# A mixing layer's triangular inverses: blocks of 16 rows on VectorE, joined to 32 by products on TensorE

## The chip, the cores and the metric

The kernel runs on one core of a Trainium2 chip. Its time is the device time of one execution in microseconds (us). All arrays are fp32. Matrix products run on TensorE (PE in the profile, PEld is its weight loading), element-wise work on VectorE (DVE), ScalarE (ACT) and GpSimd (POOL); the sync engine (SP) issues the DMAs.

## The reference, cut to what matters

Four layers, each of token mixing (two recurrent branches over 256 context and 256 latent tokens, in two directions) and a dense channel mixer. The change lies in the second branch, whose state update is a delta rule:

```python
def step(S, xt):
    w_t, k_t, b_t, kk_t, v_t = xt[:5]
    sa = -jnp.einsum('...vk,...k->...v', S, kk_t)
    S = S * w_t[..., None, :] + sa[..., None] * b_t[..., None, :] + v_t[..., None] * k_t[..., None, :]
    if not read:
        return S, None
    return S, jnp.einsum('...vk,...k->...v', S, xt[5])
```

The kernel computes it in chunks of 64 tokens. Within a chunk, each token's correction depends on all earlier ones, so each chunk needs the inverse of a 64 by 64 triangular matrix with a unit diagonal: I minus a strictly triangular part.

## The kernel before, in words

All work is first recorded as a program and then put in order by a list scheduler (`Plan.schedule`), which gives each engine a fixed order of instructions before the kernel is built, from costs and ranks of its own. On the chip each engine goes through its order strictly, so an instruction that must wait holds up everything behind it on its engine. `plan.together` keeps several matmuls in one piece of that order.

A layer has two parts. In the **mixing stage** the projections of the input (tile `p_ps`, three split products for each weight) run beside two recurrent branches. The **tail** after it (output projections and channel mixer) is nearly all products of 512 columns.

The delta-rule branch handles its 8 heads as 4 pairs p = 0 to 3. For each pair three streams are recorded:

- `rw_pair(p)` computes decays, keys and so on, and from them the triangular matrices ("ZA", in the memory of tile `AR`) and the scores (`SC`).
- `rw_solve(p)` inverts 32 matrices of a pair at once (2 directions, 8 chunks, 2 heads).
- `rw_chain(p)` goes through the 8 chunks one after another: products on `c_ps`, copies by ScalarE, state updates by VectorE (`UV<-c_ps`, `S<-c_ps`). It needs the scores and the inverses of its pair. The chain of pair p runs beside the solve of pair p + 1.

`rw_solve` cuts each 64 by 64 matrix into two diagonal blocks of 32 and one block off the diagonal. The 64 diagonal blocks (32 matrices, 2 blocks each) are laid out with one block to a partition: 64 partitions with 32 by 32 values each, in `LT` (the tile's memory is `XS`), by two transposes in blocks of 32 (`XS<-AR`). Then comes the elimination: for i = 30 down to 1 one multiplication into a scratch area in `S` (`S<-XS`) and one addition (`XS<-XS,S`) on (31 - i) x i values in each partition, 60 dependent VectorE instructions. Two transposes (`AR<-XS`) and one more (`XS<-AR`) bring the inverted blocks back, and TensorE joins the two blocks of 32 to 64 by two products of 32 by 32 per matrix (`s_ps<-AR,XS`, `s_ps<-XS,AR`), with ScalarE copies out of PSUM between them. The tag `s` of PSUM has two buffers, which the scores, the transposes and the small projections of the mixing stage share.

```python
tv = tmp[:, 0:n * i].rearrange("p (c j) -> p c j", j=i)
vec.tensor_tensor(out=tv, in0=Lp[:, i + 1:32, i:i + 1].to_broadcast([C, n, i]),
                  in1=Lp[:, i:i + 1, 0:i].to_broadcast([C, n, i]), op=ALU.mult)
vec.tensor_tensor(out=Lp[:, i + 1:32, 0:i], in0=Lp[:, i + 1:32, 0:i], in1=tv, op=ALU.add)
```

Nearly every instruction is recorded through one helper, so the profile gives line 343 for all of them; they are told apart by tiles. A product of fp32 operands shows as two matmul records in the trace.

Of the kernel before, what the change touches and what calls it, by code (L numbers as in the profile page):

```python
# [12 lines left out]
AF = mybir.ActivationFunctionType  # L13
ALU = mybir.AluOpType
# [15 lines left out]
C = 64  # L30
# [62 lines left out]
class Plan:  # L93
# [104 lines left out]
    def cost(eng, name, out, args, kw):  # L198
# [31 lines left out]
        if name == "tensor_scalar":  # L230
            if ptr:
# [7 lines left out]
               act=dict(pe=230.0, act=145.0, vec=143.0, pool=170.0, dma=200.0),  # L239
               vec=dict(pe=245.0, act=130.0, vec=127.0, pool=130.0, dma=200.0),  # L240
# [113 lines left out]
def body(ctx, tc, xT, cc, ada_w, w_in, rw_lo, rw_g2, proj_a, proj_b, w_out, ffn_w1, ffn_w2,  # L354
         vecs, lbl, c_id, c_bo, c_sc, c_hg, c_sh, out, depth=4):
    nc = tc.nc
    plan = Plan(nc, tc)
    vec, act, pool, pe, dma = plan.vec, plan.act, plan.pool, plan.pe, plan.dma
# [13 lines left out]
    def st(tag, shape, dt=F32, bufs=1):  # L372
        return plan.tile(sp, shape, dt, tag, 2 if tag in B2 else bufs, tag)
# [24 lines left out]
    def sps(tag="s"):  # L398
        return plan.tile(pss, [P, 512], F32, tag, PSB[tag], tag + "_ps")
# [344 lines left out]
    def layer(l, pm, xs, xd, hh, hl):  # L744
# [59 lines left out]
        SX = st("S", [P, 1024])  # L804
        S = SX[:, 0:512].rearrange("p (d s c) -> p d s c", d=2, s=4)
        ar3 = MX[:, 0:3072].rearrange("p (w d s c) -> p d s w c", w=3, d=2, s=NCH)
        LT = MX[:, 3072:4096]
# [177 lines left out]
        def rw_solve(p):  # L985

            yield lambda: ("za" if EA[last] else "grp", p) in flags
            yield lambda: p == 0 or ("sol", p - 1) in flags
            yield ("at", par["ps"][p] + par["pz"])
            z, o = C * (p % 2), C - C * (p % 2)  # L990
            za = ZA.rearrange("p d s h c -> p (d s h) c")
            ZZ = za[z:z + C]
            Zq = [ZZ[32 * q:32 * q + 32] for q in range(2)]
            Lp = LT[o:o + C].rearrange("p (c j) -> p c j", j=32)
            T1 = LT[z:z + 32].rearrange("p (n c) -> p n c", c=32)
            Hs = LT[z + 32:z + C].rearrange("p (n c) -> p n c", c=32)
            tmp = SX[o:o + C, 512:768]
            for q in range(2):
                vec.transpose(Lp[32 * q:32 * q + 32], Zq[q][:, :, 32 * q:32 * q + 32].rearrange("p n i -> p i n"))
            for i in range(30, 0, -1):  # L1000
                n = 31 - i
                tv = tmp[:, 0:n * i].rearrange("p (c j) -> p c j", j=i)
                vec.tensor_tensor(out=tv, in0=Lp[:, i + 1:32, i:i + 1].to_broadcast([C, n, i]),
                                  in1=Lp[:, i:i + 1, 0:i].to_broadcast([C, n, i]), op=ALU.mult)
                vec.tensor_tensor(out=Lp[:, i + 1:32, 0:i], in0=Lp[:, i + 1:32, 0:i], in1=tv, op=ALU.add)
                yield 1
            vec.memset(LT[o:o + C, 0:1024:33], 1.0)
            vec.memset(Zq[1][:, :, 0:32], 0.0)
            for q in range(2):
                vec.transpose(Zq[q][:, :, 32 * q:32 * q + 32].rearrange("p n c -> p c n"), Lp[32 * q:32 * q + 32])  # L1010
            vec.transpose(T1, Zq[0][:, :, 0:32])
            for hf in range(2):
                ps = sps()
                for i in range(16):
                    n = hf * 16 + i
                    pe.matmul(ps[z + 32:z + C, i * 32:(i + 1) * 32], Zq[0][:, n, 32:C], T1[:, n, :], start=True,
                              stop=True)
                act.activation(Hs[:, hf * 16:hf * 16 + 16, :],
                               ps[z + 32:z + C].rearrange("p (a c) -> p a c", a=16), AF.Copy)
                yield 1.5  # L1020
            for hf in range(2):
                ps = sps()
                for i in range(16):
                    n = hf * 16 + i
                    pe.matmul(ps[z:z + 32, i * 32:(i + 1) * 32], Hs[:, n, :], Zq[1][:, n, 32:C], start=True, stop=True)
                act.activation(Zq[0][:, hf * 16:hf * 16 + 16, 32:C],
                               ps[z:z + 32].rearrange("p (a c) -> p a c", a=16), AF.Copy)
                yield 1.5
            flags["sol", p] = 1
# [283 lines left out]
        for i in range(4):  # L1313
            run += [[0.0, 4 * i, f"P{i}", rw_pair(i), None], [0.0, 4 * i + 1, f"C{i}", rw_chain(i), None],
                    [0.0, 4 * i + 1.5, f"Z{i}", rw_solve(i), None],
                    [0.0, 4 * i + 2, f"H{i}", hg_head(i), None]]
# [208 lines left out]
```

## Time and profile before

| | us |
|---|---|
| median of 3 runs (4347.94 to 4358.15) | 4348.0 |
| the profiled execution, its own time | 4335.38 |
| its span, first to last instruction | 4333.6 |
| busy: PE / DVE / ACT / POOL | 3898.9 / 3248.5 / 2147.8 / 1901.6 |

The four mixing stages lie at about 60 to 660, 1205 to 1842, 2335 to 2985 and 3478 to 4060 us of the span. A PE that is busy is not one that works at its fastest, since the ends of pipelined matmuls are modelled: a second look at the time per product is needed.

### The profile page before, as it was taken

The page shows a single profiled execution, that of the slowest core. Times are in us where ns is not written, and L with a number is a line of the kernel's source. Part 1 is how long each engine was busy: PE and PEld are TensorE (multiplying, and loading weights), DVE is VectorE, ACT ScalarE, POOL GpSimd, SP SyncE. Part 2 cuts the span into 40 slices and gives each one's busy share as a digit, 9 for nine tenths or more (in the row PEclk, how much of TensorE's full clock was granted, in tenths as well). Part 3 has the DMA queues.
Part 4 walks back from the last instruction along what each step waited for, and adds up shares of the span by engine and source line. Part 5 has one row for each costly group of instructions (what it writes and reads, how often), then busy time and mean ns, then how long its engine had stood idle before and what let it go on. Part 6 is the DMA issues. An engine that isn't in the chain of part 4 may idle for free.

```text
span 4333.6 us, 71689 instructions
## 1 busy us (share of the span) xinstructions
PE 3898.9 (90%) x26290; PEld 3081.4 (71%) x26290; DVE 3248.5 (75%) x5759; ACT 2147.8 (50%) x4234; POOL 1901.6 (44%) x1622
## 2 busy tenths in 40 slices
PE   7898898799988988999998889899899987888898
PEld 4666666677776666778777767667777875676898
DVE  5988978977479899675536998987854289888665
ACT  4555653433255556534433556554444254566564
POOL 1343543456533435464553243444555433345332
PEclk8999899999998998999999989889999997798999
DMA  4211137455422111363444111116444331111555
GB/s 149 64 53 46 54 100 219 137 167 157 132 87 62 53 49 51 122 210 100 134 121 136 55 47 55 50 45 216 134 134 129 103 113 43 44 56 52 172 151 161
DMA packets 661409, 451.03 MB, mean 104 GB/s; under 512 B 28224, under 2 KB 584256, under 8 KB 661056
## 3 DMA queue, kind: packets, MB, share of 16 engines
q1 hardware_dynamic: 661056, 446.44, 34.6%
q8 instruction: 207, 3.39, 0.3%
q14 instruction: 146, 1.20, 0.1%
HBM read 416.98 MB, written 29.36 MB: 103 GB/s over the span
## 4 chain that ended last, share of the span: by engine, by line
PE 40%; DVE 18%; issue 3%; ACT 2%; DMA 1%; POOL 1%; DVEq 0%; SPq 0%; POOLq 0%; ACTq 0%
PE p_ps L343 31%; PE s_ps L343 4%; DVE XS L343 3%; PE c_ps L343 3%; PE g_ps L343 2%; DVE wl L343 2%; DVE S L343 2%; DVE AR L343 1%; DVE hX L343 1%; DVE UV L343 1%; DVE X8b L343 1%; DVE X8a L343 1%; DVE fn L343 1%; DVE y L343 1%; DVE og L343 1%
## 5 line engine op out<-in xcount | busy, mean ns | idle before, releaser
L343 PE MATMUL p_ps<-hh,wl 128*128 128x512 f32 (+1 forms) x2784 | 1057.9, 397 | 64.6 <-DVE wl L343 48.7
L343 PE MATMUL p_ps<-hh,wh 128*128 128x512 f32 (+1 forms) x2784 | 1062.5, 393 | 35.7 <-ACT wh L343 24.4
L343 PE MATMUL p_ps<-hl,wh 128*128 128x512 f32 (+1 forms) x2784 | 1055.4, 390 | 0.0
L343 ACT ACTIVATE wh<-wr 128x512 fp32r<-128x512 f32 x986 | 608.4, 621 | 812.7 <-PE p_ps L343 726.6
L343 POOL TENSOR_TENSOR wl<-wr,wh 128x512 fp32r<-128x512 f32 x492 | 673.2, 1371 | 696.5 <-ACT wh L343 501.9
L343 PEld LDWEIGHTS p_ps<-hh,wl 128*128 128x128 f32 x2784 | 539.1, 196 | 198.5 <-DVE wl L343 68.3
L343 PEld LDWEIGHTS p_ps<-hh,wh 128*128 128x128 f32 x2784 | 538.3, 196 | 144.3 <-ACT wh L343 37.0
L343 PEld LDWEIGHTS p_ps<-hl,wh 128*128 128x128 f32 x2784 | 538.9, 196 | 93.1 <-issue 6.2
L343 DVE TENSOR_TENSOR wl<-wr,wh 128x512 fp32r<-128x512 f32 (+1 forms) x494 | 364.8, 743 | 126.0 <-ACT wh L343 80.8
L343 POOL TENSOR_SCALAR fn<-fn 128x512 f32<-128x512 f32 (+1 forms) x152 | 230.9, 1519 | 249.3 <-ACT fn L343 232.2
L343 DVE TENSOR_TENSOR fn<-fn,p_ps 128x512 f32<-128x512 f32 (+1 forms) x208 | 127.4, 615 | 254.8 <-ACT fn L343 152.8
L343 POOL TENSOR_SCALAR S0P<-S,pcs 128x64 f32<-128x64 f32 x192 | 148.4, 791 | 345.1 <-DVE S L343 329.8
L343 ACT ACTIVATE fn<-fn 128x512 f32<-128x512 f32 (+1 forms) x304 | 174.4, 574 | 104.6 <-POOL fn L343 100.3
L343 POOL COPY SC<-XS 64x256 f32<-64x256 f32 x128 | 73.6, 575 | 327.7 <-DVE SC L343 321.9
L343 DVE TENSOR_TENSOR XS<-XS,S 64x30 f32<-64x30 f32 (+14 forms) x480 | 208.2, 434 | 11.3
L343 POOL TENSOR_TENSOR HB<-HB,HA 128x512 f32<-128x512 f32 x112 | 162.6, 1452 | 113.9 <-ACT hY L343 110.6
L343 DVE TENSOR_TENSOR S<-XS 64x30 f32<-64x30 f32 (+14 forms) x480 | 198.7, 414 | 11.1
L343 POOL TENSOR_TENSOR HA<-HA 128x512 f32<-128x512 f32 x112 | 144.4, 1289 | 19.7 <-ACT hX L343 14.0
L343 PE MATMUL p_ps<-SC,wh 128*128 128x512 f32 (+1 forms) x440 | 145.6, 367 | 6.4 <-ACT SC L343 4.3
L343 DVE SCALAR_TENSOR_TENSOR UV<-c_ps,pcs,S0P 64x64 f32<-64x64 f32 x384 | 108.6, 283 | 40.6 <-PE c_ps L343 31.1
L343 ACT ACTIVATE fn<-p_ps 128x512 f32<-128x512 f32 (+1 forms) x217 | 113.1, 521 | 50.9 <-PE p_ps L343 33.8
L343 POOL TENSOR_SCALAR X8a<-X8a 128x512 f32<-128x512 f32 x64 | 106.9, 1670 | 41.2 <-ACT X8a L343 38.7
(477 smaller groups left out, 8781.8 us busy)
## 6 DMA issues: line engine op xcount, KB each, us to landing
wr<-ffn_w SPq DMA_DIRECT2D x512, 256.0 KB, 3.0
wr<-w_in SPq DMA_DIRECT2D x408, 256.0 KB, 2.9
hq<-ada_w SPq DMA_DIRECT2D x242, 256.0 KB, 2.9
PB<-ada_w SPq DMA_DIRECT2D x110, 256.0 KB, 2.9
wr<-w_out SPq DMA_DIRECT2D x64, 256.0 KB, 3.3
gts<-fn SPq DMA_DIRECT2D x48, 256.0 KB, 3.1
wr<-proj_a SPq DMA_DIRECT2D x32, 256.0 KB, 3.7
wr<-proj_b SPq DMA_DIRECT2D x32, 256.0 KB, 4.2
```

The costliest lines, as they stand in the source:

```text
L343: getattr(self.eng[self.on[i]], name)(*args, **kw)
```

## The change

The elimination stops at blocks of 16 rows. Each partition's 32 by 32 block is treated as two diagonal blocks of 16, both in one instruction, by an access pattern with one more dimension (`blocks`): 14 steps of 2 x (15 - i) x i values in place of 30 of (31 - i) x i. The 16 by 16 block below the diagonal, which the elimination no longer reaches, is made by two products of 16 by 16 for each of the 64 blocks: first the block itself times one inverse, copied by ScalarE into scratch `G` (memory of `S`), then the other inverse times that, copied into the matrix. Three transposes (`S<-XS`, `XS<-XS`) lay the operands out for TensorE. A memset of a block that is already zero is dropped, and the products of the join of 32 to 64 now stand in groups (`plan.together`). The tables that steer the list scheduler are untouched, but it orders the whole new program anew.

```diff
-            for i in range(30, 0, -1):
-                n = 31 - i
-                tv = tmp[:, 0:n * i].rearrange("p (c j) -> p c j", j=i)
-                vec.tensor_tensor(out=tv, in0=Lp[:, i + 1:32, i:i + 1].to_broadcast([C, n, i]),
-                                  in1=Lp[:, i:i + 1, 0:i].to_broadcast([C, n, i]), op=ALU.mult)
-                vec.tensor_tensor(out=Lp[:, i + 1:32, 0:i], in0=Lp[:, i + 1:32, 0:i], in1=tv, op=ALU.add)
+            for i in range(14, 0, -1):
+                n = 15 - i
+                tv = tmp[:, 0:2 * n * i].rearrange("p (b c j) -> p b c j", b=2, j=i)
+                vec.tensor_tensor(out=tv, in0=blocks(i + 1, n, i, 1).to_broadcast([C, 2, n, i]),
+                                  in1=blocks(i, 1, 0, i).to_broadcast([C, 2, n, i]), op=ALU.mult)
+                vec.tensor_tensor(out=blocks(i + 1, n, 0, i), in0=blocks(i + 1, n, 0, i), in1=tv, op=ALU.add)
                 yield 1
             vec.memset(LT[o:o + C, 0:1024:33], 1.0)
-            vec.memset(Zq[1][:, :, 0:32], 0.0)
+            low = Lp[:, :, 0:16].rearrange("p i j -> p j i")
+            vec.transpose(XT.rearrange("p n j -> p j n"), low)
+            vec.transpose(G.rearrange("p (n j) -> p j n", j=16), low[:, :, ::-1])
+            vec.transpose(XB.rearrange("p n c -> p c n"), Lp[:, 16:32, ::-1])
             for q in range(2):
                 vec.transpose(Zq[q][:, :, 32 * q:32 * q + 32].rearrange("p n c -> p c n"), Lp[32 * q:32 * q + 32])
+            qs = [slice(z + 32 * q, z + 32 * q + 16) for q in range(2)]
+            rows = [slice(32 * q, 32 * q + 16) for q in range(2)]
+            ps = sps()
+            with plan.together(0.55):
+                for n in range(32):
+                    for q in range(2):
+                        pe.matmul(ps[qs[q], n * 16:n * 16 + 16], G[rows[q], n * 16:n * 16 + 16], XB[rows[q], n, :],
+                                  start=True, stop=True)
+            for q in range(2):
+                act.activation(G[rows[q]], ps[qs[q]], AF.Copy)
+            yield 1.5
+            ps = sps()
+            with plan.together(0.55):
+                for n in range(32):
+                    for q in range(2):
+                        pe.matmul(ps[qs[q], n * 16:n * 16 + 16], XT[rows[q], n, :], G[rows[q], n * 16:n * 16 + 16],
+                                  start=True, stop=True)
+            for q in range(2):
+                act.activation(Zq[q][0:16, :, 32 * q + 16:32 * q + 32],
+                               ps[qs[q]].rearrange("p (n c) -> p n c", c=16), AF.Copy)
+            yield 1.5
             vec.transpose(T1, Zq[0][:, :, 0:32])
```

**Place 1: VectorE, the end of the last solve of the second layer.** Before, the elimination's last steps lie around the last of the chain's 7 state updates (`UV<-c_ps`, all of the chain of the pair before):

```order
L343 TENSOR_TENSOR wl<-wr,wh 128x512
L343 SCALAR_TENSOR_TENSOR UV<-c_ps,pcs,S0P 64x64 x4
L343 SCALAR_TENSOR_TENSOR S<-c_ps,pcs,S0P 128x64 x2
L343 TENSOR_TENSOR hX<-hX,hq 128x512
L343 TENSOR_TENSOR XS<-XS,S 64x27x4
L343 TENSOR_TENSOR S<-XS 64x84
L343 TENSOR_TENSOR XS<-XS,S 64x28x3
L343 TENSOR_TENSOR S<-XS 64x58
```

And the same place in the changed program, where the update between the last steps is the third of that chain:

```order
L343 TENSOR_TENSOR S<-XS 64x28
L343 SCALAR_TENSOR_TENSOR UV<-c_ps,pcs,S0P 64x64 x4
L343 SCALAR_TENSOR_TENSOR S<-c_ps,pcs,S0P 128x64 x2
L343 TENSOR_TENSOR XS<-XS,S 64x2x14
L343 MEMSET XS 64x32
L343 COPY_PREDICATED SS<-hgm,g_ps 128x256
L343 STREAM_TRANSPOSE S<-XS 64x16x32
L343 STREAM_TRANSPOSE XS<-XS 64x16x32 x2
L343 STREAM_TRANSPOSE AR<-XS 32x32x32
```

The elimination is over four of the chain's steps earlier. In the order of VectorE, each of the solves 1 to 3 of the first three layers began and ended with 6 or 7 of the chain's updates in between before; now there are 2 or 3.

**Place 2: TensorE, the products of the third solve of the second layer.** Before, the join is 64 products of 32 by 32, here just behind the triangular matrices of the next pair (`s_ps<-XS,BK`):

```order
L343 MATMUL s_ps<-XS,BK 64x64 x16
L343 MATMUL s_ps<-XS,AR 32x32 x16
L343 MATMUL g_ps<-hX,hY 64x64 x8
L343 MATMUL s_ps<-XS,AR 32x32 x16
L343 MATMUL s_ps<-AR,XS 32x32 x32
L343 MATMUL g_ps<-hX,hY 64x64 x8
```

After, 128 products of 16 by 16 in two groups stand there first:

```order
L343 MATMUL s_ps<-XS,BK 64x64 x16
L343 MATMUL s_ps<-XS,S 16x16 x64
L343 MATMUL p_ps<-hh,wl 128x512
L343 MATMUL s_ps<-S,XS 16x16 x64
L343 MATMUL p_ps<-hh,wh 128x512
...
L343 MATMUL s_ps<-XS,AR 32x32 x32
```

The second group reads ScalarE's copy of the first, and here a single projection lies between the two; in the third solve of the first layer nothing does, in that of the third layer one, and in the other solves 3 to 12 rows. Twelve projections stand between the second group and the join here.

## Rows read from the trace of the kernel before

**Rows 1.** The page, parts 1 and 2: busy time of each engine; DVE in 40 slices.
```profile
PE 3898.9 (90%) x26290; PEld 3081.4 (71%) x26290; DVE 3248.5 (75%) x5759; ACT 2147.8 (50%) x4234; POOL 1901.6 (44%) x1622
DVE  5988978977479899675536998987854289888665
```

**Rows 2.** Busy time by stretch: one tail, then two mixing stages.
```profile
core 0: us, PE busy (x) PEld busy (x) DVE busy (x) ACT busy (x) POOL busy (x), PEclk, DMA share, GB/s
1842.00:2335.00 493.00, 470.03 (x2167) 379.84 (x2166) 271.40 (x371) 187.40 (x331) 269.82 (x197) 0.98 0.47 141
2335.00:2985.00 650.00, 582.37 (x4595) 442.95 (x4595) 553.25 (x1062) 366.97 (x738) 252.84 (x243) 0.90 0.23 70
3478.00:4060.00 582.00, 495.77 (x4108) 401.19 (x4107) 501.26 (x1023) 336.03 (x728) 233.09 (x242) 0.85 0.23 67
```

**Rows 3.** The chain of waits in those two mixing stages, share by engine and tile written.
```profile
by line: PE p_ps L343 29.0%; PE s_ps L343 10.9%; PE c_ps L343 7.2%; DVE XS L343 7.0%; issue 5.5%; PE g_ps L343 4.9%; DVE wl L343 4.4%; DVE S L343 3.8%; DVE X8b L343 2.5%; DVE AR L343 2.4%; DVE hX L343 2.3%; DVE X8a L343 1.9%; DVE UV L343 1.
by line: PE p_ps L343 21.9%; DVE XS L343 9.9%; PE s_ps L343 9.0%; PE c_ps L343 6.5%; issue 5.8%; DVE S L343 5.7%; DVE wl L343 4.5%; DVE AR L343 4.4%; PE g_ps L343 4.0%; DVE hX L343 2.6%; DVE UV L343 2.5%; DVE SC L343 1.8%; DVE X4c L343 1.6%
```

**Rows 4.** VectorE groups of the first of them: xcount, busy us, mean ns, idle before.
```profile
L343 DVE TENSOR_TENSOR XS<-XS,S 64x30 f32<-64x30 f32 (+14 forms) x120 | 49.9, 416 | 3.0
L343 DVE STREAM_TRANSPOSE XS<-AR 32x1024 f32<-32x1024 f32 x12 | 20.4, 1698 | 0.3
L343 DVE TENSOR_TENSOR XS<-X4c,ep 128x512 f32<-128x512 f32 x8 | 7.2, 898 | 0.2
L343 DVE TENSOR_TENSOR XS<-X8b,ep 128x512 f32<-128x512 f32 x8 | 6.3, 791 | 0.0
L343 DVE TENSOR_TENSOR S<-XS 64x30 f32<-64x30 f32 (+14 forms) x120 | 48.3, 403 | 3.0
L343 DVE SCALAR_TENSOR_TENSOR S<-c_ps,pcs,S0P 128x64 f32<-128x64 f32 x48 | 11.4, 279 | 0.6
L343 DVE MEMSET AR<- 32x1024 f32 x4 | 3.6, 912 | 1.1 <-issue 1.1
```

**Rows 5.** The elimination's additions by shape, whole run.
```profile
L343 DVE TENSOR_TENSOR XS<-XS,S 64x30 f32<-64x30 f32 x32 | 7.5, 235 | 0.7
L343 DVE TENSOR_TENSOR XS<-XS,S 64x58 f32<-64x58 f32 x32 | 8.2, 258 | 0.7
L343 DVE TENSOR_TENSOR XS<-XS,S 64x84 f32<-64x84 f32 x32 | 9.8, 308 | 0.8
L343 DVE TENSOR_TENSOR XS<-XS,S 64x108 f32<-64x108 f32 x32 | 15.4, 480 | 0.7
```

**Rows 6.** A loaded chain, an unloaded one, an elimination: first to last start.
```profile
L343 PE MATMUL c_ps<-UV,SC x64: 222/222/314, 2673.3 to 2742.8; 128*64 128x64 f32 x64
...
L343 PE MATMUL c_ps<-UV,SC x56: 222/222/270, 2925.3 to 2968.0; 128*64 128x64 f32 x56
...
L343 DVE TENSOR_TENSOR XS<-XS,S x30: 210/382/1529, 2681.4 to 2754.8; 64x30 f32<-64x30 f32 x2, 64x58 f32<-64x58 f32 x2, 64x84 f32<-64x84 f32 x2, 64x108 f32<-64x108 f32 x2
```

**Rows 7.** Busy time in those two chains and from first to last solve.
```profile
2667.00:2743.00 76.00, 66.18 (x638) 48.44 (x636) 69.97 (x141) 39.95 (x86) 33.05 (x37) 0.93 0.15 43
2920.00:2972.00 52.00, 51.97 (x442) 37.65 (x438) 32.02 (x79) 25.69 (x56) 20.52 (x18) 0.96 0.45 138
2439.00:2883.00 444.00, 393.63 (x3159) 294.99 (x3159) 398.68 (x767) 250.27 (x503) 180.24 (x174) 0.88 0.18 53
```

**Rows 8.** The projections alone: mixing stage, then tail.
```profile
2439.00:2883.00 444.00, 246.00 (x811) 154.45 (x810) 36.48 (x75) 20.64 (x34) 0.88 0.18 53
...
1842.00:2335.00 493.00, 456.00 (x2067) 368.77 (x2066) 52.87 (x88) 22.14 (x39) 0.98 0.47 141
```

**Rows 9.** Small products by shape, whole run.
```profile
L343 PE MATMUL s_ps<-XS,AR 32*32 32x32 f32 x1024 | 46.0, 209 | 9.9 <-DVE XS L343 4.6 <-DVE AR L343 3.3 <-DVE y L343 1.7
L343 PE MATMUL s_ps<-XS,BK 64*64 64x64 f32 x512 | 26.7, 277 | 19.1 <-DVE XS L343 18.8 <-DVE AR L343 0.2
```

**Rows 10.** One of the join's copies out of PSUM.
```profile
L343 ACT ACTIVATE XS<-s_ps 32x512 f32<-32x512 f32 x32 | 18.5, 588 | 42.3 <-PE s_ps L343 42.3
```

More of the change, by code (lines that the diff above doesn't have):

```diff
@@ L996, in rw_solve, with blocks @@
             Hs = LT[z + 32:z + C].rearrange("p (n c) -> p n c", c=32)
+            XT = LT[z:z + C, 0:512].rearrange("p (n c) -> p n c", c=16)
+            XB = LT[z:z + C, 512:1024].rearrange("p (n c) -> p n c", c=16)
+            G = SX[z:z + C, 512:1024]
             tmp = SX[o:o + C, 512:768]
+            def blocks(r, nr, c, nc_):
+                t = LT[o:o + C, 0:1]
+                return bass.AP(t.tensor, t.offset + 32 * r + c, [t.ap[0], [528, 2], [32, nr], [1, nc_]])
             for q in range(2):
@@ L1013, in rw_solve @@
                 ps = sps()
[L1014 to L1017, printed above, removed]
+                with plan.together():
+                    for i in range(16):
+                        n = hf * 16 + i
+                        pe.matmul(ps[z + 32:z + C, i * 32:(i + 1) * 32], Zq[0][:, n, 32:C], T1[:, n, :], start=True,
+                                  stop=True)
                 act.activation(Hs[:, hf * 16:hf * 16 + 16, :],
@@ L1022, in rw_solve @@
                 ps = sps()
-                for i in range(16):
-                    n = hf * 16 + i
-                    pe.matmul(ps[z:z + 32, i * 32:(i + 1) * 32], Hs[:, n, :], Zq[1][:, n, 32:C], start=True, stop=True)
+                with plan.together():
+                    for i in range(16):
+                        n = hf * 16 + i
+                        pe.matmul(ps[z:z + 32, i * 32:(i + 1) * 32], Hs[:, n, :], Zq[1][:, n, 32:C], start=True,
+                                  stop=True)
                 act.activation(Zq[0][:, hf * 16:hf * 16 + 16, 32:C],
```

## The prediction

> **What bounds it now.** I read the page first. TensorE is busy 90% of the span and VectorE 75% [rows 1], so by the page the added products fall on the busiest engine. But VectorE's share is a mean: in the 40 slices it stands at 8 and 9 in the mixing stages and at 5 and 6 in the tails. So I cut the span into stages next. In the mixing stage of the third layer (650 us) VectorE is busy 553.25 us; in the tail before it 271.40 of 493 [rows 2]. From first to last solve it is 398.68 of 444 us, 90% [rows 7].
>
> TensorE in that stretch is busy 393.63 us, 89%, but not at its fastest. Its projections took 246.00 us for 811 matmuls, 303 ns each, while in the tail 2067 took 456.00 us, 221 ns each at a granted clock of 0.98 [rows 8]. At the stretch's clock of 0.88 that pace is 246 ns, so 811 need 200 us: 46 us of the busy time are slack, and 50 us more are idle. VectorE is what the mixing stage has too little of, and TensorE has some 96 us to spare in 444.
>
> What a stretch costs shows best in two chains of the third layer. The chain of pair 1 runs from about 2667 to 2743 with the elimination for pair 2 beside it, whose additions start from 2681.4 to 2754.8; the last chain, with none beside it, runs from about 2920 to 2972 [rows 6]. VectorE is busy 69.97 of 76 us in the first (92%) and 32.02 of 52 in the second [rows 7]. The elimination is not all of that difference, but it is the part that this change cuts.
>
> **What goes.** In the third layer the elimination is 49.9 + 48.3 = 98.2 us of VectorE, 24.6 for each of 4 solves [rows 4]. The new one has 28 instructions of 28, 52, 72, 88, 100, 108 and 112 values, each size four times. I read their times off the additions of 30, 58, 84 and 108 values (235, 258, 308 and 480 ns [rows 5]), straight lines between: 235, 253, 285, 337, 423, 480, 500 ns, together 2.51 us, four times 10.0 us. The ends: all at 235 ns gives 6.6 us, all at the present mean of an addition, 416 ns [rows 4], gives 11.6; the unseen third dimension of the access could bring it there. I take 10.0, since these rows already hold the disturbances of a full stage: 24.6 falls to 10.0, by 59%. The memset goes too, 0.91 us [rows 4].
>
> **What is added.** VectorE: three transposes of 64 x 512. A row of 32 x 1024 takes 1.70 us [rows 4]; half as many values for each partition give 0.85 if the two groups of 32 partitions go side by side, 1.70 if not. I take 0.85, since an addition on 64 partitions pays for its values in one partition only (0.24 us for 30). With the memset, 3 x 0.85 - 0.91 = 1.6 us a solve, at most 4.2.
>
> TensorE: 128 products, 256 records a solve, 4096 in all. Single products of 32 columns took 46.0 us for 1024 records, 45 ns each; those of 64 columns, which go in pairs on different quarters of the array, 26.7 for 512, 52 ns [rows 9]. No row has 16 columns. If the pair costs by its columns, a record is 52 x 16/64 = 13 ns, 13 us a layer; if a pair takes as long as one single record of 32 columns, 22.5 ns, 23 us; if the two go one after another, 45 ns, 46 us. I take 23: the names alternate between two partition groups as those of 64 do, but the step from 64 to 32 columns shows nothing of a floor beneath.
>
> On that floor the Trainium skill speaks against the change: TensorEngine Tiling (Array Packing), section Instruction Overhead, says that a matmul of 1 column takes as long as one of 60 and warns against cutting a dimension that is already small. By that rule the price is that of 32 columns, as taken; by columns alone the sum below would be 4 x 0.53 x 10 = 21 us better. No run here shows which.
>
> ScalarE: four copies a solve of 0.588 us [rows 10], 9.4 us a layer. It is busy 366.97 of 650 us [rows 2]; where the solve isn't what the chain waits for, its idle time takes them in; where it is, they count whole.
>
> **The sum, two ways.** First by the chain of waits, with its order held. In the third layer VectorE writing XS is 7.0% of 650 us, 45.5, and writing S 3.8%, 24.7 [rows 3]. The elimination is 49.9 of the 83.8 us of groups that write XS, and 48.3 of 59.7 that write S [rows 4]: 27.1 + 20.0 = 47 us on the chain. In the fourth layer the shares are 9.9% and 5.7% of 582 us; with the same parts 34.3 + 26.8 = 61. The mean, 54 us, is 55% of the elimination. 59% of it goes: 32.1 us. Back come 55% of 4 x 1.6 on VectorE (3.6) and of ScalarE's 9.4 (5.2), and on TensorE 53% of 23 (12.3): the shares of PE on the chain, 52.0% and 41.4% [rows 3], over its busy shares of 582.37 in 650 and 495.77 in 582 [rows 2], are 0.58 and 0.49. Left are 11 us a layer, 44 in all.
>
> Second by the stretches beside a chain. There VectorE loses 24.6 - 10.0 - 1.6 = 13.0 us, at 92% busy 14.1 us of time; the 76 us would be 62, still above the 52 of the free chain. Three such chains a layer make 42 us, 170 in all, if TensorE has room. It has: of 96 us in 444, 42 go with the time and 23 are taken by new work, and 31 remain.
>
> The first leaves out that the order changes: the eliminations no longer lie across the whole chain but across 2 or 3 of its updates (place 1), so the later steps are free of them. The second leaves out waits of the new hops. I take 100 us, near the middle of 44 and 170. The profiled execution took 4335.38 us, so 4235; the median of the runs shown is 12.6 higher: **4248 us**.
>
> **Rivals.** *VectorE is all the limit.* It loses 58.2 - 6.4 = 52 us a layer; at 90% busy the stage shrinks by 58, in all 230: 4118 us. For it speaks VectorE's share, against it that TensorE would have 15 us of slack left (96 - 58 - 23). Chance 0.12.
>
> *TensorE's order stalls at the new groups (slower).* The engine goes through its order strictly, and the second group reads ScalarE's copy of the first, in three solves with nothing or one projection between (place 2); projections, scores and chain steps are queued behind it. Each group also holds one of the two `s` buffers until its copies are done. If TensorE loses each stage whole, that is 128 records x 22.5 ns + 2 x 0.588 = 4.1 us, 32 times 131 us: 4248 + 131 = 4379 us. It cancels the gain from 3.1 us a stage. For it: at the 64-column groups that wait for VectorE TensorE already idled 19.1 us [rows 9], over 16 solves 1.2 us each. Against it: in 13 of 16 solves 3 rows or more lie between, and 1.2 us a group would cost 38 us only. Chance 0.18.
>
> *No change.* The stage is set by TensorE after all, and what VectorE gives up is paid back in products: at the price for pairs one after another, 46 us a layer, the first sum is 32.1 - 3.6 - 24.6 - 5.2 = -1 us: 4348 us. For it the page's 90%, against it the 303 ns. Chance 0.10.
>
> **Chances and range.** The forecast, from 44 to 170 us of gain (4304 to 4178 us, its own range), has 0.60. With the first rival faster is 0.72; no change, within 0.3% (13 us, about what a measurement of this kernel can tell), 0.10; slower 0.18. The range goes a little past the second sum, to 4160, and half way into the slower rival, to 4365; it leaves out some 0.10 below and 0.09 above.
>
> **What would show it.** Right: VectorE's groups S<-XS and XS<-XS,S near 40 us a layer in place of 98, chains beside a solve near 62 us, mixing stages some 25 us shorter each, the tails unchanged. The new products near 92 us over the run, the new transposes 0.85 us. Wrong: PE idle before `s_ps<-S,XS` above 1.2 us each time, records of 16 columns at 45 ns, transposes at 1.7, or the last chain of a layer ending as late as now with projections still to do behind it.

## The result: slower by 1.3%

The changed kernel took 4408.0 us (median of 4 runs, 4403.4 to 4409.5), the kernel before, beside it, 4353.1 (4 runs, 4347.9 to 4359.2): ratio 1.0131, 95% interval 1.0117 to 1.0145. The forecast was 4248 with a range to 4365, so sign and range are both wrong. The profiled execution has a span of 4405.6 us against 4333.6.

The page of the changed kernel, parts 1 and 2, to be held against [rows 1]:

```profile
PE 3952.6 (90%) x30386; PEld 3146.6 (71%) x30386; DVE 3037.1 (69%) x5283; ACT 2185.7 (50%) x4298; POOL 1840.0 (42%) x1618
DVE  5876868977378768568445877667775187877665
```

VectorE lost 211 us of work and TensorE gained 54, much as intended; the time still grew, by 55 us of the medians and 72 us of span (the profiled execution of the kernel before lay 18 us below the median beside the changed kernel). Where it grew is seen by stretch: the tail after the second layer's mixing, then the mixing stages of the third and fourth layers, as in [rows 2].

```profile
core 0: us, PE busy (x) PEld busy (x) DVE busy (x) ACT busy (x) POOL busy (x), PEclk, DMA share, GB/s
1871.00:2385.00 514.00, 490.45 (x2235) 394.45 (x2234) 295.30 (x391) 197.37 (x350) 277.12 (x200) 0.98 0.48 144
2385.00:3034.00 649.00, 573.66 (x5549) 445.61 (x5548) 478.16 (x927) 367.37 (x737) 226.75 (x236) 0.88 0.20 62
3551.00:4124.00 573.00, 494.68 (x5077) 400.63 (x5075) 447.59 (x894) 341.56 (x736) 223.57 (x240) 0.86 0.23 67
```

The third layer's mixing stage is as long as before (649 for 650 us) with 75 us less VectorE work in it, and the tail is 21 us longer (514 for 493). The fourth layer's stage is 9 us shorter. By the first split of each layer's input (`hh<-fn`, at 55.3, 1233.5, 2369.1 and 3512.6 us before, at 58.5, 1260.1, 2417.8 and 3584.9 after), the first three layers each take 22 to 24 us more and the fourth as long as before.

Why a longer tail? The projections alone in that tail, [rows 8] for before, and in the next mixing stage:

```profile
1871.00:2385.00 514.00, 475.78 (x2135) 383.39 (x2134) 53.20 (x88) 23.82 (x42) 0.98 0.48 144
2385.00:3034.00 649.00, 353.29 (x1369) 242.82 (x1368) 54.53 (x118) 30.24 (x50) 0.88 0.20 62
```

The tail has 2135 of them in place of 2067: projections that were not done in the mixing stage. Before, the third mixing stage had 1439, now 1369; of the 70 that are missing, 63 are done in the tail behind it (2136 for 2073). The place where they went missing is the chain of pair 1. The projections of the changed kernel ahead of that chain, beside it, and behind it (third layer), and then all engines in the middle stretch:

```profile
2655.00:2714.00 59.00, 37.26 (x134) 25.47 (x133) 7.12 (x18) 3.12 (x5) 0.94 0.23 69
2714.00:2797.00 83.00, 0.00 (x0) 0.00 (x0) 0.00 (x0) 0.00 (x0) 0.66 0.02 4
2797.00:2830.00 33.00, 21.85 (x74) 14.06 (x74) 7.64 (x19) 3.23 (x5) 0.88 0.19 59
...
2714.00:2797.00 83.00, 55.13 (x734) 46.67 (x725) 49.28 (x111) 32.36 (x74) 28.45 (x37) 0.66 0.02 4
```

For 83 us not one projection starts; in the same chain of the kernel before there were 119, 38.67 us:

```profile
2667.00:2743.00 76.00, 38.67 (x119) 21.91 (x119) 2.12 (x3) 1.79 (x3) 0.93 0.15 43
```

TensorE is busy only 55 of 83 us with the chain's and the first branch's small products, its granted clock falls to a mean of 0.66, VectorE is busy 49 of 83, and weights come in at 4 GB/s. Nobody is short of anything but order. What stands behind the gap is seen in ScalarE's copies that take projections out of PSUM (timeline, start and duration in us), and in who reads the tile `X8b` at that time:

```profile
2713.36 0.60 ACT L343 ACTIVATE he<-p_ps 128x512 f32<-128x512 f32 x1
2797.51 0.68 ACT L343 ACTIVATE X8b<-p_ps,lmu 128x512 f32<-128x512 f32 x1
2799.36 0.69 ACT L343 ACTIVATE X8b<-p_ps,lmu 128x512 f32<-128x512 f32 x1
2813.01 0.58 ACT L343 ACTIVATE og<-p_ps 128x512 f32<-128x512 f32 x1
...
L343 PE MATMUL s_ps<-ident,X8b x8: 421/421/476, 2766.1 to 2796.6; 128*128 128x128 f32 x8
L343 ACT ACTIVATE X8b<-p_ps,lmu x2: 681/684/687, 2797.5 to 2799.4; 128x512 f32<-128x512 f32 x2
```

Two projections of each pair go to `X8b`: in this layer they are copied there at 2436 and 2462 us for pair 0, at 2538 and 2550 for pair 1, at 2660 and 2673 for pair 2, so those at 2797.5 and 2799.4 are pair 3's. No projection matmul lies between 2714 and 2797, so theirs were done ahead of the gap and stood in PSUM until `X8b`, with the values of pair 2 in it, had been read for the last time, at 2796.6. These last reads are the second half of pair 2's scores and transposes, which wait for the chain of pair 1, since they write over the scores that it still reads:

```profile
2793.14 0.69 PE L343 MATMUL c_ps<-SC,UV 128*64 128x64 f32 x16 [0.78 <-ACT UV L343]
2793.74 1.29 DVE L343 TENSOR_TENSOR SC<-s_ps,scm 128x512 f32<-128x512 f32 x2 [0.45 <-PE c_ps L343]
2795.86 1.12 PE L343 MATMUL s_ps<-ident,X8b 128*128 128x128 f32 x4
```

The copies of pair 3 begin 0.9 us after that, and only then do projections flow again. The longest times between two projection matmuls are 76.7, 89.3 and 88.9 us, one in each of the first three layers; before, none was above 20.4.

The chain itself is quicker, against [rows 6]. The first two rows are the changed kernel's, the last one is the kernel before:

```profile
L343 PE MATMUL c_ps<-S,AR x64: 218/311/366, 2725.2 to 2792.1; 64*64 64x64 f32 x64
L343 PE MATMUL c_ps<-UV,SC x64: 222/314/369, 2732.7 to 2795.6; 128*64 128x64 f32 x64
...
L343 PE MATMUL c_ps<-S,AR x64: 218/218/366, 2666.7 to 2739.0; 64*64 64x64 f32 x64
```

With the solve for pair 2 beside it, `c_ps<-UV,SC` took 63 us from first to last start where it took 70, and the chain as a whole, from its first `c_ps<-S,AR` to its last `c_ps<-UV,SC`, 70 where it took 76. What the change promised for VectorE came; TensorE's filling went.

### The profile page after: what moved, and what is told of

It reads as the page before. It is cut to its first block, busy times and chain, and to the rows that moved or that the text cites. A ratio compares the mean times of both kernels' runs of the same rounds, so it can differ in the third digit from the quotient of the medians.

```text
span 4405.6 us, 79578 instructions
## 1 busy us (share of the span) xinstructions
PE 3952.6 (90%) x30386; PEld 3146.6 (71%) x30386; DVE 3037.1 (69%) x5283; ACT 2185.7 (50%) x4298; POOL 1840.0 (42%) x1618
## 4 chain that ended last, share of the span: by engine, by line
PE 61%; DVE 23%; issue 6%; ACT 4%; DMA 3%; POOL 2%; SPq 0%; DVEq 0%; POOLq 0%; ACTq 0%
PE p_ps L343 45%; PE s_ps L343 8%; PE c_ps L343 4%; PE g_ps L343 3%; DVE XS L343 3%; DVE og L343 2%; DVE wl L343 2%; DVE vt L343 2%; DVE S L343 1%; DVE AR L343 1%; DVE UV L343 1%; DVE X8a L343 1%; DVE X8b L343 1%; DVE y L343 1%; DMA hq<-ada_w 1%
## 5 line engine op out<-in xcount | busy, mean ns | idle before, releaser
L343 POOL TENSOR_SCALAR S0P<-S,pcs 128x64 f32<-128x64 f32 x192 | 127.4, 676 | 330.0 <-DVE S L343 329.2
L343 POOL TENSOR_TENSOR HB<-HB,HA 128x512 f32<-128x512 f32 x112 | 152.1, 1358 | 143.9 <-ACT hY L343 140.9
L343 POOL COPY SC<-XS 64x256 f32<-64x256 f32 x128 | 64.5, 504 | 336.4 <-DVE SC L343 330.3
L343 PEld LDWEIGHTS c_ps<-UV,SC 128*64 128x64 f32 x1024 | 78.5, 152 | 77.2 <-issue 53.0
L343 PE MATMUL c_ps<-UV,SC 128*64 128x64 f32 x1024 | 96.0, 242 | 41.1 <-DVE S L343 34.2
L343 DVE TENSOR_TENSOR hX<-hX,hq 128x512 f32<-128x512 f32 x128 | 105.8, 826 | 37.1 <-ACT hX L343 35.4
```

What stands on the lines that cost most here:

```text
L343: getattr(self.eng[self.on[i]], name)(*args, **kw)
```

## How the recording decides it

A layer's streams are recorded one piece at a time. Each has a position, `yield n` moves it on by n, a function it yields holds it until a flag is set, and the stream of the lowest position goes next:

```python
run.sort(key=lambda r: r[0:2])
for r in run:
    if r[4] is None or r[4]():
        break
```

Tiles with one buffer are given out in this order, so a use that is recorded early holds its place even where it must wait long. The elimination yields 1 for each step: 30 before, 14 now. In the first three layers the second solve (pair 1's) ends at position 268 before and at 255 now. Head 0 of the first branch ends at 260, and heads 1 and 2, with their projections (`he`, `og`, `hq`), can go on only then. Before, head 0 came first. Now the solve does: it releases the chain of pair 1, this releases the second half of pair 2, and this pair 3 and its `X8b` projections, which are all recorded ahead of the projections of heads 1 and 2. In the fourth layer another row of the table sets the positions, and there is no such swap.

## The experiments

The first eight were planned under three theories. T1: TensorE sets the time, so VectorE's relief is worth nothing and each added product counts. T2: the new order is the loss. T3: the two new stages lie on the path ahead of each chain. The last four tell the swap (T-gate) from a general change of pace.

**e1_double**, the order of the changed kernel, each product of 16 by 16 issued twice (`mark` is a label on the recorded instructions, "J16" for these products, "C16" for their copies, "far" in e3 for the steps left out):

```diff
+                for name, args, kw in self.nodes[i].calls * (2 if mark == "J16" else 1):
```

> The changed kernel in its own order, each group of 16 by 16 products issued twice (same operands, same result): 2048 more products, 59.9 us of TensorE by the changed kernel's trace. Theory 1, TensorE sets the time and VectorE's relief is worth nothing: 4408 + 60 = 4468 us. Theory 2, the new order as such is the loss (the scheduler's tables fitted the old program): most of the products hide in its gaps, 4408 to 4430. Theory 3, the two new stages lie on the path just ahead of each chain: 4468 as well, so this run tells theory 2 from the others.

Measured: 4535.4 us, 1.0443 (1.0424 to 1.0462) of before, some 135 us above the changed kernel. More than twice the 60 us that these products take once, and above what any of the three theories gave; e8 shows why this is no price for one of them.

**e2_after_no16**, the order of the changed kernel, without its products of 16 by 16 and their copies:

```diff
+                if mark in ("J16", "C16"):
+                    continue
```

> The changed kernel in its own order, without both groups of 16 by 16 products and without their copies by ScalarE (the off-diagonal blocks of 16 are left out, so this part of the inverse isn't computed). Theory 1: the 60 us of TensorE go, 4348, level with before. Theory 2: the order stays, so 4380 to 4408. Theory 3: products, copies and hops go from the path, 16 times about 8 us, 4280, and VectorE's relief shows below before.

Measured: 4345.4 us, 1.0010 (1.0001 to 1.0020). Even with none of the added work of TensorE and ScalarE, this order only draws level with the kernel before. That is T1's number, not T2's; T1 falls with the next run. The gaps without projections are still there: 78.5, 87.1 and 88.1 us.

**e3_before_short**, the order of the kernel before, the elimination's steps i = 30 to 15 left out:

```diff
+                plan.mark = "far" if i > 14 else None
...
+                if mark == "far":
+                    continue
```

> The kernel before in its own order, the elimination steps i = 30 to 15 left out (28 of 60 instructions stay; the inverses are incomplete): VectorE has about 14 us less in each of 16 solves, nothing is added and nothing moves. Theory 1: no change, 4353 within 13 us. Theories 2 and 3: VectorE's relief is worth something when it costs nothing, 4353 less 50 to 150.

Measured: 4269.3 us, 0.9827 (0.9811 to 0.9843): 75 us faster by the ratio, 72 by the medians. VectorE's groups in it, whole run:

```profile
L348 DVE TENSOR_TENSOR XS<-XS,S 64x238 f32<-64x238 f32 (+6 forms) x224 | 96.0, 428 | 5.5
L348 DVE TENSOR_TENSOR S<-XS 64x238 f32<-64x238 f32 (+6 forms) x224 | 89.1, 398 | 5.3
```

They were 208.2 and 198.7 us in the kernel before, so 222 us of VectorE's work are worth 75 us when the order is held. T1 falls.

**e4_before_groups**, the kernel before with the join's products in groups and without the memset, ordered anew:

```diff
-            vec.memset(Zq[1][:, :, 0:32], 0.0)
...
+                with plan.together():
```

> The kernel before with only the two small edits of the change: the products of the join of 32 to 64 in groups, and without the memset of a block that is already zero. The scheduler orders it anew. Theory 2, the time hangs on the order: it moves by 0.5% or more either way. Theories 1 and 3: within 0.3% of 4353.

Measured: 4323.9 us, 0.9962 (0.9949 to 0.9975). These two parts of the change help a little and are not the loss. A gain of 0.4% lies between what T2 and its rivals gave, so it tells none of them apart. The changed kernel and all its variants hold these two parts too.

**e5_after_pace**, the changed kernel with the pace of the old elimination in the recording; the instructions are the same:

```diff
-                yield 1
+                yield 30 / 14
```

> The changed kernel with one number changed: each of the 14 elimination steps counts 30/14 in the stream's own pace (yield) in place of 1, so that what follows a solve is recorded as late among the other streams as it was with 30 steps. The instructions are the same, and so is their work; the scheduler orders them anew. Theory 2, named closer now (the loss is the earlier recorded place of what follows the elimination): from 4398 beside this chip's before of 4341 to 4320 or below, a gain of 70 us or more. Theories 1 and 3: within 15 us of the changed kernel.

Measured: 4331.8 us, 0.9972 (0.9960 to 0.9984), 12 us above the 4320 that T2 gave. The whole loss is gone and no gap is above 19.3 us. T2 stands; T3 falls, since the new stages are all still there.

**e6_before_pace**, the reverse on the kernel before, with no work changed:

```diff
-                yield 1
+                yield 14 / 30
```

> The kernel before with the opposite edit: each of its 30 elimination steps counts 14/30. No instruction is added, taken or resized. Theory 2: slower by 50 us or more. Theories 1 and 3: no change, since no engine has other work.

Measured: 4414.2 us, 1.0161 (1.0138 to 1.0184), with gaps of 84.9, 90.8 and 74.0 us. The loss comes without the change.

**e7_pace_no16**, e5 without the products of 16 by 16 and their copies (marks as in e2):

> As e5 in its order, but the 16 by 16 products and ScalarE's copies of them are left out (that part of the inverse isn't computed). In an order that is not the bound by itself the products cost between nothing and their own 60 us of TensorE: 0 to 60 us below e5. If they stand on the path with their hops (theory 3) it is 80 or more.

Measured: 4298.0 us, 0.9892 (0.9869 to 0.9915). By the ratios (0.9972 less 0.9892) products and copies cost 35 us in this order; by those of the changed kernel and e2 (1.0131 less 1.0010) 53 in the other, each uncertain by some 10 us.

**e8_pace_double**, e5 with those products twice (as in e1):

> As e5 in its order, each 16 by 16 product issued twice. In the changed kernel's own order this cost 137 us for 60 us of TensorE. If that was the order, it costs 60 or less here; if small products cost more than their busy time whatever the order (clock, queue behind them), again well over 100.

Measured: 4471.7 us, 1.0295 (1.0269 to 1.0322), 140 us above e5. The groups of e8 (busy, mean ns, idle before), the second group in e5, and one group of e8 in TensorE's timeline:

```profile
L346 PE MATMUL s_ps<-S,XS 16*16 16x16 f32 x4096 | 60.9, 180 | 26.2 <-issue 25.9
L346 PE MATMUL s_ps<-XS,S 16*16 16x16 f32 x4096 | 58.4, 176 | 27.8 <-issue 24.6 <-DVE AR L346 3.3
...
L343 PE MATMUL s_ps<-S,XS 16*16 16x16 f32 x2048 | 29.9, 175 | 1.0 <-issue 1.0
...
211.10 2.63 PE L346 MATMUL s_ps<-XS,S 16*16 16x16 f32 x197
215.22 0.98 PE L346 MATMUL s_ps<-XS,S 16*16 16x16 f32 x59 [1.48 <-issue]
```

After 197 records TensorE stands for 1.48 us and waits for nothing that the profile shows. Such stops make 50 us over the run, where e5 has 1.0. With the 60 us of work they are 110 of the 140 us; the other 30 are not settled. A doubled group is thus dearer than two groups, and e1 and e8 do not price the change.

**e9_head_early** and **e10_head_edge**, the changed kernel with one number of a table altered, the position from which head 0 is recorded:

```diff
-         hs=(37, 101, 193, 247), hn=28.2, hl=23.9, gs=52.2, gd=53.8),
+         hs=(31, 101, 193, 247), hn=28.2, hl=23.9, gs=52.2, gd=53.8),
```

> The changed kernel with one number of a table altered: head 0 of the first branch is recorded from position 31 instead of 37 in the first three layers; no instruction is added or taken away. In the changed program the second solve ends at position 255 of the recording, and head 0 ends at 260; before the change the solve ended at 268, behind it. The end of head 0 lets heads 1 and 2 and their projections be recorded. T-gate: what costs the time is that one swap. With it the chain and the next pair's projections (X8b) are recorded ahead of head 1, and these projections cannot leave PSUM until the tile X8b is read for the last time, so that TensorE has no projection for some 80 us in each of three layers. At 31 head 0 ends at 254, ahead of the solve: the projections he, og, hq and fn stand ahead of X8b again and the time falls to 4325 to 4350 us. T-pace, the rival: it is the earlier place of all that follows an elimination, in four solves of each layer, that costs; this undoes one of them, and the time stays within 20 us of the changed kernel's 4408.

```diff
+         hs=(33, 101, 193, 247), hn=28.2, hl=23.9, gs=52.2, gd=53.8),
```

> The same with 33 in place of 37: head 0 moves by 4 of the 6 positions of the run above, and ends at 256, just behind the second solve's 255. T-gate: the swap stays, so nothing is gained: 4395 to 4415 us, and the gap without projections is there. If head 0's own place mattered by its distance, two thirds of the gain of the run above would be had, some 4360. T-pace: 4400.

Measured: 4335.4 us for 31, 0.9988 (0.9970 to 1.0005), and 4405.5 for 33, 1.0151 (1.0136 to 1.0166). Two positions of one stream (33 to 31) make 70 us, four (37 to 33) nothing: it is the swap, not the distance. For 31, the copies out of PSUM around the chain of pair 1 in the third layer, and its projections:

```profile
2691.59 0.59 ACT L343 ACTIVATE he<-p_ps 128x512 f32<-128x512 f32 x1
2701.17 0.59 ACT L343 ACTIVATE hq<-p_ps 128x512 f32<-128x512 f32 x1
2704.06 0.60 ACT L343 ACTIVATE he<-p_ps 128x512 f32<-128x512 f32 x1
2737.12 1.26 ACT L343 ACTIVATE X8b<-p_ps,lmu 128x512 f32<-128x512 f32 x2
...
2674.00:2740.00 66.00, 38.55 (x125) 21.57 (x125) 5.70 (x11) 3.04 (x5) 0.97 0.16 45
```

And for 33, all of its projections in that chain:

```profile
2715.00:2799.00 84.00, 0.00 (x0) 0.00 (x0) 2.69 (x7) 1.86 (x3) 0.64 0.02 4
```

With 31, `he`, `hq` and `he` leave PSUM ahead of `X8b` and 125 projections fill the chain; with 33 none.

**e11_before_head_late**, the kernel before with head 0 from 46:

```diff
-         hs=(37, 101, 193, 247), hn=28.2, hl=23.9, gs=52.2, gd=53.8),
+         hs=(46, 101, 193, 247), hn=28.2, hl=23.9, gs=52.2, gd=53.8),
```

> The kernel before with 46 in place of 37 in the same table: head 0 ends at 268 or 269, behind the second solve's end at 268; the work is that of the kernel before. T-gate: the swap alone, without any of the changed work, costs 50 to 75 us: 4395 to 4420 us, and X8b leaves PSUM ahead of he, og and hq in the first three layers. T-pace: head 0 comes 9 positions later and no solve moves; within 15 us of the kernel before, 4330 to 4365.

Measured: 4382.9 us, 1.0102 (1.0086 to 1.0117): 43 us slower, 12 us short of what T-gate expected and 18 us above what the rival did. `X8b` again leaves PSUM ahead of `og` in all of the first three layers, but the gaps are shorter. The one of the second layer:

```profile
1562.00:1609.00 47.00, 0.00 (x0) 0.00 (x0) 2.61 (x7) 1.37 (x2) 0.64 0.02 7
```

The swap costs time without the change as well. Its gaps (20.8, 47.9 and 29.0 us) are shorter since the last `he` leaves PSUM later: 25 to 48 us behind the first product of the chain, where in the changed kernel it leaves 8 to 12 us ahead of it. Why was not followed up.

**e12_after_tuned**, the changed kernel with seven numbers of its tables altered:

```diff
-    dict(ps=(7, 46.8, 55, 71), pg=1.1, pn=6.3, pc=87.2, pz=185.1,
-         hs=(37, 101, 193, 247), hn=28.2, hl=23.9, gs=52.2, gd=53.8),
+    dict(ps=(7, 46.8, 55, 71), pg=1.1, pn=5.7, pc=87.2, pz=185.1,
+         hs=(30, 101, 193, 247), hn=28.2, hl=23.9, gs=52.2, gd=53.8),
...
-    dict(ps=(2, 96.8, 165.6, 261), pg=5.4, pn=14.5, pc=160.8, pz=94.6,
+    dict(ps=(2, 96.8, 165.6, 261), pg=5.4, pn=14.5, pc=157.3, pz=94.6,
...
-    dict(P=0, Z=-10000.0, C=21000.0, H=0, G=-477000.0, A=0),
-    dict(P=0, Z=10000.0, C=738000.0, H=2000.0, G=-53000.0, A=-20000.0),
+    dict(P=0, Z=-10000.0, C=21000.0, H=4075.0, G=-480980.0, A=0),
+    dict(P=0, Z=-14784.0, C=738000.0, H=2000.0, G=-108233.0, A=-20000.0),
```

> The changed kernel with seven numbers of its tables altered: head 0 from 30, pn 5.7, bias of H 4075 and of G -480980 in the first three layers; pc 157.3, bias of Z -14784 and of G -108233 in the last. No instruction is added or taken away. T-gate and the sum of the terms: with the swap undone and the order set anew for this work the change is worth what VectorE's relief gave in the old order (72 us), less the 34 us that the products and copies cost: 4300 to 4325 us, below both kernels. The rival, that the changed work has no order in which it beats the one before: 4340 or more.

Measured: 4298.4 us, 0.9909 (0.9894 to 0.9924), 2 us under the range that was expected and faster than both kernels. The tables of the kernel before were not set anew in the same way, so this shows that the changed work can win, not that it wins by 0.9% against the best order of the old.

**By layers.** The profiled executions, from the first `hh<-fn` of the first layer to that of the fourth, and from there to the end (us):

| kernel | layers 1 to 3 | layer 4 |
|---|---|---|
| before | 3457 | 821 |
| changed | 3526 | 821 |
| e5, changed with the old pace | 3479 | 786 |
| e6, before with the new pace | 3517 | 838 |
| e9, changed with head 0 from 31 | 3451 | 832 |
| e10, changed with head 0 from 33 | 3528 | 818 |
| e12, changed with seven numbers | 3457 | 789 |

The swap shows where the table makes it: from e10 to e9 the first three layers lose 77 us, and the fourth gains 14. The old pace does more than undo it: e5 takes 47 us from the first three layers and 35 from the fourth, which has no swap, and what e12 has over e9 lies wholly in the fourth. So the order moves the fourth layer too, between 786 and 838 us here, by causes that were not followed up, and that e5 and e9 end so close is in part luck.

## Why the prediction was wrong, step by step

**The step that failed** is the one that chose between the two sums: "The first leaves out that the order changes", counted as a help because the chain's "later steps are free of them". It saw rightly that the eliminations end over four chain steps earlier, and the chains did become quicker. What it did not ask is who else is recorded by the same clock: everything behind an elimination moved forward as well, past the end of head 0. By the runs, the change of order is a loss of some 70 us (70 from e9 to e10, by the swap alone; 69 from e5 to the changed kernel and 69 for e6, by the whole pace), where the forecast had made it a gain of 56 over the first sum's 44. On the chain of waits VectorE gave way to the projections (third and fourth layers, against [rows 3]):

```profile
by line: PE p_ps L343 35.1%; PE s_ps L343 13.9%; PE c_ps L343 8.2%; PE g_ps L343 5.9%; DVE XS L343 4.9%; issue 4.1%; DVE wl L343 2.5%; DVE AR L343 2.3%; DVE X8a L343 2.1%; DVE S L343 2.0%; DVE UV L343 1.9%; DVE hX L343 1.3%; ACT UV L343 1.3
by line: PE p_ps L343 28.3%; PE s_ps L343 13.1%; PE c_ps L343 6.4%; DVE XS L343 6.4%; issue 5.2%; DVE wl L343 3.5%; PE g_ps L343 3.4%; DVE AR L343 3.1%; DVE S L343 2.9%; DVE UV L343 2.6%; DVE X8b L343 2.1%; DVE X8a L343 1.6%; DVE hX L343 1.
```

In the third layer writing `XS` and `S` fell from 10.8% to 6.9% of the chain, and `p_ps` rose from 29.0% to 35.1%, by 39 us, though fewer projections ran in that stage.

**What bounds it.** That VectorE is short in the mixing stages was right: e3. The exchange rate, a second step, was not. The first sum had 55% of the elimination on the path; e3 gave 75 us for 222, 34%.

**VectorE's terms.** The third layer's groups, against [rows 4]:

```profile
L343 DVE STREAM_TRANSPOSE XS<-AR 32x1024 f32<-32x1024 f32 x12 | 20.3, 1694 | 15.8 <-PE s_ps L343 11.2 <-ACT AR L343 4.5
L343 DVE TENSOR_TENSOR XS<-XS,S 64x28 f32<-64x28 f32 (+6 forms) x56 | 16.3, 291 | 1.8
...
L343 DVE TENSOR_TENSOR S<-XS 64x28 f32<-64x28 f32 (+6 forms) x56 | 14.2, 253 | 1.7
L343 DVE STREAM_TRANSPOSE XS<-XS 64x512 f32<-64x512 f32 x8 | 8.4, 1064 | 0.1
L343 DVE STREAM_TRANSPOSE S<-XS 64x512 f32<-64x512 f32 x4 | 4.5, 1124 | 0.1
```

The elimination takes (16.3 + 14.2) / 4 = 7.6 us a solve; 10.0 was taken, with 6.6 as the lower end. The transposes take 1.06 and 1.12 us where 0.85 was taken: between the two bounds, near the lower. Together VectorE got 1.7 us a solve more relief than forecast.

**TensorE's and ScalarE's terms**, whole run, against [rows 9, 10]:

```profile
L343 PE MATMUL s_ps<-S,XS 16*16 16x16 f32 x2048 | 30.7, 177 | 4.4 <-issue 2.7 <-ACT S L343 1.6
L343 PE MATMUL s_ps<-XS,S 16*16 16x16 f32 x2048 | 29.2, 175 | 3.3 <-DVE AR L343 2.9 <-issue 0.4
...
L343 ACT ACTIVATE S<-s_ps 16x512 f32<-16x512 f32 x32 | 18.8, 587 | 39.1 <-PE s_ps L343 38.7
...
L343 ACT ACTIVATE AR<-s_ps 16x512 f32<-16x512 f32 x32 | 18.6, 580 | 0.4
```

A record of 16 columns took 59.9 us / 4096 = 14.6 ns, 15 us a layer in place of 23: close to the 13 ns by columns. The rule of the Trainium skill that spoke against the change (TensorEngine Tiling (Array Packing), section Instruction Overhead) speaks of a product's latency; read as its price, as the prediction read it, it would have made it that of 32 columns, 22.5 ns. The trace does not bear that reading out for products that go in pairs. ScalarE's copies cost what was taken. Products and copies together cost 35 us in a good order and 53 in the bad one, where 4 x (12.3 + 5.2) = 70 was taken.

**The rivals.** The slower one had the sign and nearly the size (4379) by another mechanism: TensorE stood 4.4 us in all before the 16 second groups, 0.28 us each, of which 1.6 us in all for ScalarE's copies, while it needed more than 1.2 each. VectorE as the whole limit, 4118, was far off. No change comes closest to what the work is worth in the old pace, but its mechanism, 46 us of products a layer, did not: they took 15.

**The signs named.** The groups `S<-XS` and `XS<-XS,S` near 40 us: 30.5. Chains beside a solve near 62 us from 76: 70 by the same ends. Mixing stages 25 us shorter: 1 and 9. Tails unchanged: 21 us longer, with 68 more projections. The sign that was named for being wrong, a last chain that ends as late as now with projections still to do behind it, is the one that came: counted from the first `hh<-fn` of its layer, the last chain ended at 590, 594, 603 and 535 us before and at 596, 595, 599 and 528 after.

**A sum by what was measured**, order held, as an estimate: the elimination fell from 406.9 to 129.1 us over the run, 278 us, more than the 222 that e3 took out, which at 34% is -94; products and copies +35; the new transposes less the memset (50.7 - 14.6 = 36 us, at 34%) +12: -47 us. The three orders without the swap gave -5 (e9, with an interval that holds no change), -12 (e5) and -40 (e12); the spread between them is the order's again (from e9 to e12 wholly the fourth layer's).

**Open** is what stopped the projections behind those for `X8b`. By the recording, `p_ps` has four buffers that go round, and the projections follow each other as pair 3's three, head 1's `he`, then its `og`, which gets the buffer of pair 3's first. That fits the trace: `he` leaves PSUM at 2713.4, projections start again at 2801.4, with pair 3's first being copied out from 2797.5, and `og` leaves at 2813.0. But no run changed the number of buffers, and the loads of weights, which stop too, were not taken apart from it.

## What to carry to other kernels

Where an order is made from recorded streams, a pace in the recording is part of the order: shorten a piece of work and everything that it releases moves forward, though nobody edited it. Before forecasting, list which streams the shortened one now overtakes, and whether what comes forward can get its tile; here products that came early but could not be put away stood in front of those that could. Then price the change twice, with the old pace kept and with the new one, since here the pace alone made some 70 us, and the changed work gained between 5 and 40 without the swap.

## What was not expected of the hardware

TensorE's granted clock fell to 0.66, a mean of stretches at 2.4 and at 1.2 GHz, in the 83 us in which it had only small products, 55 us of them, and was 0.97 in the same chain of e9 with 125 projections between them. The chain's own products are slower in it too, a median of 314 ns for `c_ps<-UV,SC` where [rows 6] have 222. Small products in pairs started every 13 ns or so in a group, but in e8 all but one of the 32 groups of 256 records stopped for 1.3 to 2.5 us after some 130 to 250 of them, with no wait that the profile names; in those of 128 records such stops came to 1.0 us in the whole run of e5 and 3.1 in that of the changed kernel.
